# Values products of edge key blocks: 64 moved queries per head instead of 128, and a new order of the products in each stay

## The chip, the cores and the metric

The kernel runs on one core of a Trainium2 chip. The metric is device time in microseconds (us) of one execution; of several runs the median counts. The core has a matmul engine (PE in the profile; its weight loads are listed apart as PEld), VectorE (DVE), ScalarE (ACT), GpSimd (POOL) and SyncE (SP), which issues most of the DMA transfers.

## The reference

The program is a two-layer encoder over 2048 positions (prompt) and 512 positions (sample), 1024 channels, fp32. Layer 0 is windowed attention with 16 heads of 64 channels and 4 key/value heads, layer 1 a Fourier mixer; both are gated and projected, and a last RMSNorm follows. The change is in layer 0 alone. Cut to what it touches:

```
WINDOW = 128; BLOCK = 128
qb = q.reshape(b, nb, BLOCK, N_KV_HEADS, GROUP, HEAD_DIM)
kw = band_windows(k, nb)            # previous, own and next key block
vw = band_windows(v, nb)
rel = kj - BLOCK - qi               # kj in 0..383, qi in 0..127
band = np.abs(rel) <= WINDOW
scores = jnp.where(mask, scores * scale + bias, -jnp.inf)
p = jnp.exp(scores - m)
p = p / denom
o = jnp.einsum('bnhgqk,bnkhd->bnqhgd', p, vw)
```

A query block of 128 sees three key blocks (two at the ends of a sequence). The band leaves weights of zero in the first and the last of them: key j of the previous block is reached by queries 0 to j only, key j of the next block by queries j to 127 only. So the lower 64 keys of the previous block have weights other than zero only for the lower 64 queries, and the upper 64 keys of the next block only for the upper 64 queries.

## The kernel before, in words

The five chunks of 512 tokens (`CHUNKS`, line 48) are worked one after the other: first the sample, then the four of the prompt. In a chunk, layer 0 goes over 8 pairs of heads (p), and for each over two pairs of query blocks (b = 0 and 2). All products work in two parts: a number is split into a high part (rounded to the matmul's input form, `F32R`) and a low part, and a product is high x high + high x low + low x high. Where both operands have 64 rows, two products run side by side, one on rows 0 to 63 of the array and one on rows 64 to 127, writing to different PSUM banks. Such a pair is called a slot here.

For one pair of query blocks the attention steps are: scores (L650), bias and minimum on VectorE (L669), exponentials on ScalarE (L677), division (L690, L692, L696), transposes of the weights into PSUM (`transp`, L709), their split into a high part (`high`, L722, ScalarE, into `pts[:, 0]`) and a low part (`low`, L726, VectorE, into `pts[:, 1]`), the values products (`values`, L750, into `av`), and the sum of the two heads' halves (L770, L780), the gate and the split of the result (L786 to L795).

`values(b)` makes the list of products. For a query block i and a key block kb in `k0..k1` there is one for the high part of the weights and one for the low part; the values v stand with both their parts beside each other as 128 weight columns (64 channels high, 64 low), and the moving operand is `pts[rows, part, i, kb]`: 64 keys, 2 heads x 128 queries = 256 columns. The order of the list is kb ascending, high and then low in each. `half(False)` is the first stay: rows 0 to 63 of the array take all products of block 0, rows 64 to 127 all products of block 1, in turn. `half(True)`, the second stay, swaps the blocks, so that each block gets its other 64 keys; ahead of it `swapped` waits until the first stay has left the banks. A stay has 6 slots where both blocks have three key blocks. The last pair of each chunk (p = 7, b = 2) uses `whole` (L758), 128 rows at a time, and has no stays.

What stands around the stays is set by hand: `PERIOD` (line 36) and, for the first chunk, `FIRST` (line 42) list the steps of one period of two query blocks, and `seq`/`pe` chain the instructions of an engine in that order. On PE a period is AV1 (first stay), T0 (transposes of another pair of blocks), AV2 (second stay), S1 (scores), A (a run of projection products, `beside`, L524, 512 columns each), T1, S2, B (projections again). AV1 uses what `lo1`, the second low part, wrote late in the period before. `pts` has one buffer (`bufs=1`), so the next `hi0` waits for the second stay.

Of the kernel before, what the change touches and what calls it, by code (L numbers as in the profile page):

```python
# [55 lines left out]
def encoder(  # L56
# [17 lines left out]
    av = spsum.tile([P, 2, 512], F32, name="av")  # L74
# [126 lines left out]
    def pe(ins):  # L201
        return seq(PE, ins) if PE in chain else ins

    def attention_phase():

        with ExitStack() as es:
# [167 lines left out]
            vblk, k_splits = {}, []  # L374
# [151 lines left out]
            def swapped(places):  # L526

                before = []
                for last, h in places:
                    if last[1 - h] is not None:  # L530
                        before.append(last[1 - h])
                        last[1 - h] = None
                if before:
                    wait = pe(PE.nop())
                    for ins in before:
                        tc.add_manual_dep(wait.ins, ins.ins.name, DONE, reason="other rows of a bank")
# [73 lines left out]
            def attention(c, p, res, uTs):  # L610

                tok, lo_t, hi_t = CHUNKS[c]
                g = p // 2
# [24 lines left out]
                def span(b):  # L638
                    gb = tok // P + b
                    k0 = 1 if tok + b * P == lo_t else 0  # L640
                    k1 = 2 if tok + (b + 1) * P == hi_t else 3
                    return gb, k0, k1
# [85 lines left out]
                def values(b):  # L728

                    pts = st.pop("pts")  # L730
                    products, last = [], [[None, None], [None, None]]
                    for i in range(2):
                        gb, k0, k1 = span(b + i)
                        for kb in range(k0, k1):
                            v = vblk[gb - 1 + kb][:, g].rearrange("p a d -> p (a d)")
                            for part in range(2):
                                pt = pts[:, part, i, kb].rearrange("p h q -> p (h q)")
                                products.append((i, v, pt))
                    by_block = [[m for m in products if m[0] == i] for i in range(2)]

                    def half(swap):
                        todo = by_block[::-1] if swap else by_block
                        if swap:
                            swapped([(last[1], 0), (last[0], 1)])
                        for n in range(max(map(len, todo))):
                            for h in range(2):
                                if n < len(todo[h]):
                                    i, v, pt = todo[h][n]
                                    rows = slice(64 * h, 64 * h + 64)
                                    last[i][h] = pe(PE.matmul(  # L750
                                        av[:, i, :256], v[rows], pt[rows], start=not swap and n == 0,
                                        stop=swap and n == len(todo[h]) - 1, skip_group_check=True,
                                    ))

                    def whole():
                        for i, todo in enumerate(by_block):
                            for n, (_, v, pt) in enumerate(todo):
                                pe(PE.matmul(  # L758
                                    av[:, i, :256], v, pt, start=n == 0, stop=n == len(todo) - 1, skip_group_check=True
                                ))  # L760

                    st["half"] = half
                    return whole
# [42 lines left out]
                for b in (0, 2):  # L806
                    one, two = sorted((b, b + 1), key=width)
                    act = one if not c or one == b else two

                    def av1(b=b):  # L810
                        st["whole"] = values(b)
                        if (p, b) == (7, 2):
                            st.pop("half")
                            st.pop("whole")()
                        else:
                            st["half"](False)

                    def gate(b=b):
                        st["split", b] = gated(b)

                    ops[b] = {
                        "S1": lambda one=one: scores(one), "S2": lambda two=two: scores(two),
                        "b1b": lambda one=one: biased(one, 1, True), "b1a": lambda one=one: biased(one, 0, False),
                        "b2a": lambda two=two: biased(two, 0, True), "b2b": lambda two=two: biased(two, 1, False),
                        "e1a": lambda one=one: exps(one, 0), "e1b": lambda one=one: exps(one, 1),
                        "e2a": lambda two=two: exps(two, 0), "e2b": lambda two=two: exps(two, 1),
                        "r1": lambda one=one: invert(one), "r2": lambda two=two: invert(two),
                        "m1a": lambda one=one: divide(one, 0, False), "m1b": lambda one=one: divide(one, 1, True),
                        "m2a": lambda two=two: divide(two, 0, False), "m2b": lambda two=two: divide(two, 1, False),
                        "T0": lambda one=one: transp(one, 0), "T1": lambda two=two: transp(two, 1),  # L830
                        "hi0": lambda one=one: high(one), "hi1": lambda two=two: high(two),
                        "lo0": lambda one=one: low(one), "lo1": lambda two=two: low(two),
                        "AV1": av1, "AV2": second_half, "t2": lambda b=b: upper(b), "add": lambda b=b: sums(b),
                        "mul": gate, "sp": lambda b=b: split_high(b), "lop": lambda b=b: split_low(b),
                    }
# [226 lines left out]
            for c in range(len(CHUNKS)):  # L1062
# [89 lines left out]
                for n in range(19):  # L1152
# [12 lines left out]
                    order = [a for a in (PERIOD if c else FIRST) if n < 15 or a[0] not in ("hi0", "lo0")]  # L1165
# [1110 lines left out]
```

## Time and profile before

| what | value |
|---|---|
| runs | 1563.36, 1567.52 and 1564.77 us; median 1564.77 us |
| the profiled execution's own time | 1567.89 us |
| its span, first to last instruction | 1566.1 us |
| granted PE clock, mean | 0.995 of full speed |
| PE busy | 1545.2 us, 99% |
| PEld busy | 1350.9 us, 86% |
| VectorE / ScalarE / GpSimd busy | 72% / 57% / 29% |
| values products in two stays (L750) | 1680 |

The profile's page gives the busy time of each engine, then the span in 40 slices, the DMA queues, the chain of work that ended last, and groups of equal instructions with their count, their busy time, the mean duration of one, and the idle time of the engine just before them. The durations of one matmul overlap: a product is listed with 0.28 us, although the next one may start 0.12 us after it. So what a product costs is read from start to start, or from the pieces of the chain, not from its mean. PEld lies beside PE: the next weights are loaded while a product still moves its columns.

### The profile page before, as it was taken

The numbers are of one execution on the slowest core, as the hardware profiler recorded it, in microseconds if no ns is written. First come the engines' busy times: TensorE is split into PE (matmuls) and PEld (weight loads), VectorE is DVE, ScalarE is ACT, GpSimd is POOL, SyncE is SP. The second block draws the span as 40 slices with busy tenths as digits, with TensorE's granted clock in tenths as the row PEclk, the third lists the DMA queues.
The fourth block names the chain that finished last, engine by engine and source line by source line (L and its number), as shares of the span: only waits on it lengthen the run. The fifth ranks groups of instructions, "written<-read, shape, count | busy, mean of one in ns | idle before, by whom it ended". The sixth has DMA issues, their size and how long they took to land.

```text
span 1566.1 us, 33658 instructions
## 1 busy us (share of the span) xinstructions
PE 1545.2 (99%) x13150; PEld 1350.9 (86%) x13150; DVE 1123.7 (72%) x2431; ACT 889.5 (57%) x1921; POOL 450.7 (29%) x616
## 2 busy tenths in 40 slices
PE   9999999999999999999999999999999999899998
PEld 7899888999898888988888899988888888788886
DVE  5888655777637776367764577767888877889896
ACT  6788534787337784257861477746656554333353
POOL 2565662421414313314214142222112111101100
PEclk9999999999999999999999999999999999999999
DMA  9677687684856765866749666675666679456852
GB/s 330 232 264 234 222 336 280 216 293 161 297 218 220 243 232 204 302 210 205 251 136 363 232 206 224 243 257 181 223 234 218 220 242 409 149 202 250 298 191 94
DMA packets 100729, 372.70 MB, mean 238 GB/s; under 512 B 11235, under 2 KB 22251, under 8 KB 83420
## 3 DMA queue, kind: packets, MB, share of 16 engines
q1 hardware_dynamic: 82716, 297.38, 54.8%
q0 software_dynamic: 16688, 70.04, 11.5%
q10 hardware_dynamic: 1168, 3.15, 0.6%
q8 instruction: 103, 1.69, 0.4%
q14 instruction: 54, 0.44, 0.1%
HBM read 280.06 MB, written 90.47 MB: 237 GB/s over the span
## 4 chain that ended last, share of the span: by engine, by line
PE 88%; DVE 6%; DMA 3%; ACT 2%; issue 1%; POOL 0%; POOLq 0%; ACTq 0%; DVEq 0%; SPq 0%
PE pj L524 27%; PE av L750 7%; PE W L134 6%; PE pj L134 6%; PE tp L134 5%; PE av L134 5%; PE spt L650 5%; PE spt L134 4%; PE tp L709 3%; PE Wo L134 3%; PE fo L134 3%; PE Z L134 3%; PE z L1385 2%; PE Zo L134 2%; PE ABp L134 2%; PE X L134 1%
## 5 line engine op out<-in xcount | busy, mean ns | idle before, releaser
L524 PE MATMUL pj<-h,wg 64*128 64x512 f32 x1920 | 440.3, 390 | 0.0
L524 PE MATMUL pj<-h,wq 64*128 64x512 f32 x1560 | 380.4, 390 | 1.3 <-DVE qab L568 1.3
L524 PEld LDWEIGHTS pj<-h,wg 64*128 64x128 f32 x1920 | 331.5, 185 | 22.6
L524 PEld LDWEIGHTS pj<-h,wq 64*128 64x128 f32 x1560 | 285.4, 185 | 22.9 <-DVE qab L568 2.7
L669 DVE CUSTOM_DVE_ANT_0 S<-spt,b 128x385 f32<-128x385 f32 (+1 forms) x320 | 165.0, 525 | 94.1 <-PE spt L650 89.7
L677 ACT ACTIVATE S<-S 128x385 f32<-128x385 f32 (+1 forms) x320 | 189.2, 592 | 62.1 <-DVE S L669 40.5
L722 ACT CAST pts<-tp 128x768 fp32r<-128x768 f32 (+1 forms) x160 | 121.3, 758 | 96.6 <-PE av L750 59.8
L726 DVE TENSOR_TENSOR pts<-tp,pts 128x768 fp32r<-128x768 f32 (+1 forms) x160 | 144.1, 901 | 14.1 <-ACT pts L722 13.4
L750 PE MATMUL av<-pts,v 64*128 64x256 f32 x1680 | 143.7, 287 | 3.0 <-DVE pts L726 3.0
L750 PEld LDWEIGHTS av<-pts,v 64*128 64x128 f32 x1680 | 127.3, 186 | 7.3 <-DVE pts L726 3.8
L795 POOL TENSOR_TENSOR uT<-o,uT 128x256 fp32r<-128x256 f32 x75 | 56.7, 756 | 244.5 <-ACT uT L791 244.2
L650 PE MATMUL spt<-kwin,qab 64*128 64x384 f32 (+1 forms) x960 | 121.4, 339 | 0.9 <-DVE S L669 0.7
L134 PE MATMUL fo<-wo,tTu 128*128 128x512 f32 x480 | 115.7, 395 | 0.0
L134 PEld LDWEIGHTS fo<-wo,tTu 128*128 128x128 f32 x480 | 89.4, 190 | 18.1
L709 PEld LDWEIGHTS tp<-ident,S 64*128 64x128 f32 x1792 | 93.1, 137 | 10.1 <-DVE pts L726 3.1
L709 PE MATMUL tp<-ident,S 64*128 64x64 f32 x1792 | 98.0, 224 | 0.1
L786 POOL TENSOR_TENSOR o<-o,s 128x256 f32<-128x256 f32 x75 | 55.6, 742 | 120.3 <-DVE o L780 95.0
L692 DVE TENSOR_SCALAR S<-S 128x384 f32<-128x384 f32 (+1 forms) x192 | 88.5, 489 | 0.1
L650 PEld LDWEIGHTS spt<-kwin,qab 64*128 64x128 f32 x960 | 85.1, 188 | 3.8 <-issue 1.8
L279 DVE SCALAR_TENSOR_TENSOR h<-xk,g0s,h 128x512 fp32r<-128x512 f32 x40 | 45.3, 1146 | 51.3 <-ACT h L278 51.1
L524 PE MATMUL pj<-wo,uT 64*128 64x512 f32 x360 | 74.8, 390 | 0.0
L278 ACT ACTIVATE h<-xk,g0s 128x512 fp32r<-128x512 f32 x40 | 28.7, 724 | 75.2 <-POOL xk L274 75.1
(376 smaller groups left out, 3355.8 us busy)
## 6 DMA issues: line engine op xcount, KB each, us to landing
wo<-wsd SPq DMA_DIRECT2D x32, 1024.0 KB, 5.9
wq<-wsd SPq DMA_DIRECT2D x31, 1024.0 KB, 6.5
wg<-wsd SPq DMA_DIRECT2D x31, 1024.0 KB, 5.8
x<-x1d SPq DMA_DIRECT2D x40, 512.0 KB, 3.8
b<-b21d SPq DMA_DIRECT2D x40, 512.0 KB, 4.7
b<-rowd SPq DMA_DIRECT2D x40, 384.0 KB, 4.2
xs<-in_x_dram SPq DMA_DIRECT2D x23, 512.0 KB, 6.2
s2d<-gt POOLq DMA_DIRECT2D x40, 256.0 KB, 4.2
```

Source lines behind the costliest of these rows:

```text
L134: ins = pe(PE.matmul(out, a[i], b[j], start=start and i + j == 0, stop=stop and i == 1, skip_group_check=more))
L524: out.last[h] = pe(PE.matmul(out.ps, a[i], b[j], **out.flags()))
L650: pe(PE.matmul(spt[j][:, 2 + k0 * P : 2 + k1 * P], res["q"][rows, qp, b * P : (b + 1) * P], kwin[g][rows, kp, b * P + k0 * P : b * P + k1 ...
L669: seq(DVE, DVE.tensor_tensor_reduce(out=s[:, e0:e1], in0=ps[:, 1 + e0 : 1 + e1], in1=st["bias"][:, j, 386 - e1 : 386 - e0][:, ::-1], scale ...
L677: last_exp[0] = seq(ACT, ACT.activation(s[:, e0:e1], s[:, e0:e1], AF.Exp, bias=s[:, 386:387], scale=-1.0, accum_out=s[:, 387:388]))
L692: seq(DVE, DVE.tensor_scalar(s[:, ks], s[:, ks], den, None, ALU.mult))
L709: pe(PE.transpose(ps[h][:, kb, j, :], s[rows, j, 1 + kb * P : 1 + (kb + 1) * P], ident[rows, rows]))
L722: seq(ACT, ACT.copy(hi, ps))
L726: seq(DVE, DVE.tensor_tensor(lo, ps, f32(hi), ALU.subtract))
L750: last[i][h] = pe(PE.matmul(av[:, i, :256], v[rows], pt[rows], start=not swap and n == 0, stop=swap and n == len(todo[h]) - 1, skip_group_ ...
L786: eng.tensor_tensor(o, o, s, ALU.mult)
L795: low = eng.tensor_tensor(lo, o, f32(hi), ALU.subtract)
```

## The change

The list `by_block` stays for `whole`. The stays use a new list, `reached(i, h)`, for block i on row half h. Three things differ.

The key block whose 64 keys of this half reach only half of the queries (`edge`: the previous block for the lower half, the next block for the upper half) moves 2 heads x 64 queries = 128 columns, in two pieces of 64, and writes only those columns of `av`. All other products are as before. The new order is: own block high, edge high, far high, far low, edge low, own low. With it the edge products of both halves stand in the same slot where both blocks have three key blocks. And the first product of a stay, which starts the accumulation, is always one of 256 columns.

```diff
+                    def reached(i, h):
+
+                        gb, k0, k1 = span(b + i)
+                        edge, far = 2 * h, 2 - 2 * h
+                        order = [(1, 0), (edge, 0), (far, 0), (far, 1), (edge, 1), (1, 1)]
+                        rows = ahead = slice(64 * h, 64 * h + 64)
+                        out = []
+                        for kb, part in order:
+                            if k0 <= kb < k1:
+                                v = vblk[gb - 1 + kb][rows, g].rearrange("p a d -> p (a d)")
+                                pt = pts[rows, part, i, kb].rearrange("p h q -> p (h q)")
+                                to = av[:, i, :256]
+                                if kb == edge:
+                                    pt = pts[rows, part, i, kb][:, :, ahead]
+                                    to = to.rearrange("p (h q) -> p h q", h=2)[:, :, ahead]
+                                out.append((i, to, v, pt))
+                        return out
+
                     def half(swap):
-                        todo = by_block[::-1] if swap else by_block
+                        todo = [reached(h ^ swap, h) for h in range(2)]
...
-                                    i, v, pt = todo[h][n]
-                                    rows = slice(64 * h, 64 * h + 64)
+                                    i, to, v, pt = todo[h][n]
                                     last[i][h] = pe(PE.matmul(
-                                        av[:, i, :256], v[rows], pt[rows], start=not swap and n == 0,
+                                        to, v, pt, start=not swap and n == 0,
```

The number of instructions is the same on every engine, and only PE's order differs. Of the 1680 products in stays 540 are edge products; 360 of these stand in 90 stays with 6 slots and three key blocks on both sides, two slots of each stay with an edge product on both halves (180 slots); the other 180 are in the 60 stays at an end of a sequence, where the two halves have lists of unequal length.

The first place is PE, head pair 2 of the second prompt chunk, first stay. The names are the output bank pair `av`, the transposed weights `pts` and the values block `v`; the shape is what is moved through the 128 output columns. Before:

```order
L750 MATMUL av<-pts_2_0_7133,v_3_3439 128x256 [waits DVE_49,Activation_49]
L750 MATMUL av<-pts_2_0_7133,v_4_3466 128x256 [waits Activation_49]
L750 MATMUL av<-pts_2_0_7133,v_3_3439 128x256
L750 MATMUL av<-pts_2_0_7133,v_4_3466 128x256 [waits DVE_49]
L750 MATMUL av<-pts_2_0_7133,v_4_3466 128x256
L750 MATMUL av<-pts_2_0_7133,v_5_6365 128x256
```

And now, in the same place:

```order
L767 MATMUL av<-pts_2_0_7133,v_4_3466 128x256 [waits DVE_49,Activation_49]
L767 MATMUL av<-pts_2_0_7133,v_5_6365 128x256 [waits Activation_49]
L767 MATMUL av<-pts_2_0_7133,v_3_3439 128x2x64
L767 MATMUL av<-pts_2_0_7133,v_6_6368 128x2x64
L767 MATMUL av<-pts_2_0_7133,v_5_6365 128x256
L767 MATMUL av<-pts_2_0_7133,v_4_3466 128x256
L767 MATMUL av<-pts_2_0_7133,v_5_6365 128x256
L767 MATMUL av<-pts_2_0_7133,v_4_3466 128x256 [waits DVE_49]
L767 MATMUL av<-pts_2_0_7133,v_3_3439 128x2x64
```

The second wait for VectorE, that for the second block's low part, stood at the fourth product and stands at the eighth; the two edge products make up the second slot.

The second place is PE in the first chunk, head pair 2, first stay, at the beginning of the sample, where block 0 has only two key blocks. Before:

```order
L750 MATMUL av<-pts_2_0_1225,v_16_433 128x256 [waits DVE_49,Activation_49]
L750 MATMUL av<-pts_2_0_1225,v_16_433 128x256 [waits Activation_49]
L750 MATMUL av<-pts_2_0_1225,v_16_433 128x256
L750 MATMUL av<-pts_2_0_1225,v_16_433 128x256 [waits DVE_49]
L750 MATMUL av<-pts_2_0_1225,v_17_438 128x256 x4
```

And now:

```order
L767 MATMUL av<-pts_2_0_1225,v_16_433 128x256 [waits DVE_49,Activation_49]
L767 MATMUL av<-pts_2_0_1225,v_17_438 128x256 [waits Activation_49]
L767 MATMUL av<-pts_2_0_1225,v_17_438 128x256
L767 MATMUL av<-pts_2_0_1225,v_18_443 128x2x64
L767 MATMUL av<-pts_2_0_1225,v_17_438 128x256
L767 MATMUL av<-pts_2_0_1225,v_16_433 128x256 x2
L767 MATMUL av<-pts_2_0_1225,v_16_433 128x256 [waits DVE_49]
```

Here too the wait moves from the fourth product to the eighth, and the edge product of the upper half stands beside a product of 256 columns.

## The prediction

> **What bounds the kernel now.** I read the page first, then the waits of PE, then the chain and the timeline of one steady period, then the chain around the longest wait. The page's head and a few of its groups:
>
> ```profile
> span 1566.1 us, 33658 instructions
> PE 1545.2 (99%) x13150; PEld 1350.9 (86%) x13150; DVE 1123.7 (72%) x2431; ACT 889.5 (57%) x1921; POOL 450.7 (29%) x616
> ...
> PEclk9999999999999999999999999999999999999999
> ...
> L524 PE MATMUL pj<-h,wg 64*128 64x512 f32 x1920 | 440.3, 390 | 0.0
> ...
> L709 PEld LDWEIGHTS tp<-ident,S 64*128 64x128 f32 x1792 | 93.1, 137 | 10.1 <-DVE pts L726 3.1
> L709 PE MATMUL tp<-ident,S 64*128 64x64 f32 x1792 | 98.0, 224 | 0.1
> ```
>
> PE is busy for 99% of the span at the full clock, and VectorE, the next one, for 72%. So time is won where PE's slots get shorter or a wait of PE goes, and nowhere else. The row of the page on the values products shows an idle time of 3.0 us in front of all 1680; the waits of PE say how it is spread:
>
> ```profile
> L750 PE MATMUL av<-pts,v 64*128 64x256 f32 x1680 | 143.7, 287 | 3.0 <-DVE pts L726 3.0
> L750 PEld LDWEIGHTS av<-pts,v 64*128 64x128 f32 x1680 | 127.3, 186 | 7.3 <-DVE pts L726 3.8
> ```
>
> ```profile
> PE av L750 <- DVE pts L726: 3.0, 3, 1.4
> PE pj L524 <- DVE qab L568: 1.3, 4, 0.4
> ```
>
> Three waits, 1.4 us at most, for the low part that L726 writes. There is no fourth. For the price of a slot the 287 ns of the group row are of no use, as durations overlap; the pieces of the chain and the timeline of a steady period (the first column is the start, the second the time) give it. First the chain, then the timeline:
>
> ```profile
> 800.12 2.75 PE pj L524 x24
> 802.87 0.71 PE av L750 x12
> 803.58 0.37 PE tp L709 x12
> 803.96 0.79 PE av L750 x12
> ```
>
> ```profile
> 802.71 0.88 PE L750 MATMUL av<-pts,v 64*128 64x256 f32 x12
> 803.42 0.53 PE L709 MATMUL tp<-ident,S 64*128 64x64 f32 x12
> 803.76 0.96 PE L750 MATMUL av<-pts,v 64*128 64x256 f32 x12
> 804.56 0.69 PE L650 MATMUL spt<-kwin,qab 64*128 64x384 f32 x6
> 805.09 1.55 PE L524 MATMUL pj<-wo,uT 64*128 64x512 f32 x12
> ```
>
> Two products make a slot. Twelve slots of 512 columns take 2.75 us, 0.229 each; three of 384 take 805.09 - 804.56 = 0.53, 0.177 each; six of 256 take 0.71, 0.118 each; six transposes of 64 columns take 0.37, 0.062 each. The first three lie on a line of 0.055 us for 128 columns. The line alone would put a slot of 128 columns at 0.063.
>
> **What a short slot costs.** Each product also loads 128 weight columns of its own. In the timeline of the projections, the loads of the next slot start together with the products of the slot before it, one slot ahead and no more:
>
> ```profile
> 799.96 0.39 PE L524 MATMUL pj<-h,wg 64*128 64x512 f32 x1
> 799.96 0.18 PEld L524 LDWEIGHTS pj<-wo,uT 64*128 64x128 f32 x1
> ...
> 800.19 0.39 PE L524 MATMUL pj<-h,wg 64*128 64x512 f32 x1
> 800.19 0.18 PEld L524 LDWEIGHTS pj<-wo,uT 64*128 64x128 f32 x1
> ```
>
> So a slot that moves few columns may end before the next weights are in. Two places of the trace bound that load.
>
> The first is the joint of T0 and AV2, where a product of 64 columns stands ahead of a values product. From the first transpose to the first score are 804.56 - 803.42 = 1.14 us. In them lie five transposes of 0.062 (0.31), six values slots of 0.118 (0.71), and what is left, 1.14 - 0.31 - 0.71 = 0.12, is the last transpose's slot. It is twice as long as the others, though it moves the same 64 columns: what follows it is a load for a values product. That is why the second stay takes 0.79 in the chain where the first takes 0.71. By this row an edge slot costs 0.12, as much as a slot of 256.
>
> The second is the length of the loads. The smallest load of this form in the trace is that of the bias rows:
>
> ```profile
> L356 PEld LDWEIGHTS pj<-ohr,rbs 33*16 33x16 f32 x2 | 0.1, 90 | 0.4 <-issue 0.4
> ```
>
> With 16 columns it lasts 90 ns, a values load with 128 lasts 186: 96 ns for 112 columns, 0.86 ns a column, so 0.110 us for 128. The loads of the transposes (137 ns for as many columns) are cheaper, which is why their slots reach 0.062. By this estimate an edge slot costs 0.110 and saves 0.008.
>
> The Trainium skill states a rule that speaks against this change: in "TensorE: Matmul & The Clock Gate", section "LDWEIGHTS (loading the stationary operand)", a load takes the number of its columns divided by 1.2, in ns, whatever the rows. That is an estimate of 107 ns here, near the 110 of the two load rows, and the trace agrees for the values loads; for the transposes' loads it does not, since 137 ns against 186 for the same columns cannot both follow it. By the page's figure an edge slot would save 0.011 us, 3.0 us over 270 slots.
>
> **The change part by part.** Edge products: 540 of 1680 move 128 columns instead of 256. As two row halves work side by side, they are 540 / 2 = 270 slots at most; 180 of them have an edge product on both halves for certain, and only such a slot can get shorter. The gain lies between nothing (0.12 a slot, the joint) and 270 x 0.008 = 2.2 us (0.110 a slot). The joint is the nearer row: the same load, in the same place, behind a product that is even shorter. I take a quarter of the upper end, 0.5 us. All of it would be on the path, as PE is never idle in these stays. The two pieces of 64 columns in what is read and written could cost something; the transposes write 64 columns at a time at 0.062 a slot, so I put that at nothing, and its bound by the slack of the load: an edge slot has 0.118 - 0.063 = 0.055 us that its columns don't need.
>
> The order: the second wait for the low part moves from the fourth product to the eighth. In the steady period nothing waits there, as the first stay's 0.71 is six whole slots; the move buys nothing. It counts in the three waits. The timeline and the chain around the first of these:
>
> ```profile
> 68.78 0.45 PE L750 MATMUL av<-pts,v 64*128 64x256 f32 x3
> 70.56 0.61 PE L750 MATMUL av<-pts,v 64*128 64x256 f32 x5 [1.34 <-DVE pts L726]
> ```
>
> ```profile
> 67.81 0.32 DVE o L780
> ...
> 68.59 0.04 DVE S L669
> ...
> 69.07 0.56 DVE S L669 x3
> 69.64 0.88 DVE pts L726
> 70.52 0.04 issue
> 70.56 0.61 PE av L750 x5
> ```
>
> Three products are out, then PE stands for 1.34 us until VectorE has done its sums, two biased scores and the low part, and seven of the stay's ten products are left. Now seven go ahead of the wait, and three are left behind it. VectorE's end at 70.52 doesn't move, since its order is the same. So four products, two slots, go from behind the wait to under it: 2 x 0.118 x 3 waits = 0.7 us. The ends: nothing, if the transposes or scores that follow wait for VectorE in turn (it is what is late there), and 3.0 us, all the waits, which seven products instead of three can't cover. I take 0.7. The first product of a stay still waits for the high parts of both blocks, as before, and what stands behind it on PE is the same; no wait is added, and no other engine has another instruction or another order. In the second stay nothing is late: it needs the same low parts.
>
> Sum: 0.5 + 0.7 = 1.2 us. Against the profiled execution's own 1567.9 us (span 1566.1 and 1.8 around it) that is 1566.7; the median of the runs shown, 1564.8, lies 3.1 below that execution, so the forecast for the median is 1563.6 us. That is 0.08% less. About 0.3%, 4.7 us, is what a measurement of this kernel can tell from no change: the three runs alone spread over 4.2 us.
>
> **Rival one: columns set the slot, so it is faster.** If the weights of an edge slot's successor come in early enough, the line through 0.229, 0.177 and 0.118 holds down to 128 columns: 0.063 instead of 0.118, and 180 to 270 slots x 0.055 = 9.9 to 14.9 us. With 0.7 for the order that is 1549.2 to 1554.2, about 1551.7. For it speaks how straight the line is, and that transposes do run at 0.062 with a load each. Against it speak the joint's 0.12 and the 186 ns of the values' loads. It decides from 0.10 us a slot downward, where 270 slots save 4.9 us. The Trainium skill has a middle way, in the page named above, section "Back-to-back issue gap": a stream of loads and products of 128 columns in a real kernel takes about 81 ns each. As an estimate that is 0.037 less a slot and up to 10.0 us, 1554.1 with the order; no row here shows such a slot.
>
> **Rival two: a short product is not moved at the full rate, so it is slower.** Every fp32 product of this form in the trace moves 256 columns or more; none shows what 128 do. If a shorter one is done in four passes, an edge slot moves 4 x 128 = 512 column steps and costs what a slot of 512 costs, 0.229, that is 0.111 more: 180 to 270 slots x 0.111 = 20.0 to 30.0 us, 1584.1 to 1594.1 with the order, about 1589. For it speaks a little that the short transposes last longer than the line of durations says: 390 - 287 = 103 ns for 256 columns leaves 184 fixed, so 64 columns take 224 - 184 = 40 ns, 0.63 ns a column against 0.40. Against it: at 0.63 ns 128 columns take 81 ns, still hidden under a load of 110, and nothing in the rows changes its rate between 256 and 512. It decides from a slot of 0.118 + 4.7 / 270 = 0.135 us upward. The Trainium skill, "FP8 and Floating Point Precision", section "TensorE Precision Notes", knows both forms, fp32 cut to fewer bits and full fp32 in four passes; it ties neither to the number of columns, and no run here shows the four passes.
>
> **How the numbers follow.** The forecast (the load holds an edge slot at 0.11 to 0.12) gets 0.69, rival one 0.15, rival two 0.16. The forecast's own range is 1559.6 (2.2 for the slots and 3.0 for the waits) to 1568, the highest of the three runs, since a single median can lie there. It holds 0.69; with rival one it holds 0.84, so the range goes from 1549 to 1568 and leaves rival two out. Faster by over 0.3%: 0.15. Within 0.3%: 0.69. Slower: 0.16.
>
> **What would show it.** In the profile after, the groups of the values products split into 256 and 128 columns. Right: a full first stay in a steady period still takes 0.69 to 0.72 us from its first product to the first transpose, and the loads still last about 186 ns. Rival one: that stay takes 0.71 - 2 x 0.055 = 0.60. Rival two: 0.71 + 2 x 0.111 = 0.93. The order is right if the three waits for L726 are still there, each about 0.2 us shorter, with seven products ahead of them; it is wrong if they have gone, or if T0 behind them waits as much longer. A stay outside 0.67 to 0.75 makes the prediction wrong.

## The result and the profile after

The changed kernel ran at a median of 1560.07 us (eight runs, 1558.37 to 1561.51), the kernel before beside it at 1564.95 (1563.16 to 1567.52). The medians differ by 4.9 us, where 1.2 us had been forecast, and the ratio over all runs is 0.9964, 95% interval 0.9954 to 0.9974. Two more comparisons below give 0.9978 and 0.9969.

The two profiled executions differ by more, 8.7 us of span. The page after, its head and the groups that answer to those of before:

```profile
span 1557.4 us, 33658 instructions
PE 1540.8 (99%) x13150; PEld 1344.4 (86%) x13150; DVE 1126.1 (72%) x2431; ACT 889.8 (57%) x1921; POOL 450.9 (29%) x616
...
L767 PE MATMUL av<-pts,v 64*128 64x256 f32 (+1 forms) x1680 | 140.9, 284 | 2.3 <-DVE pts L726 2.3
L767 PEld LDWEIGHTS av<-pts,v 64*128 64x128 f32 x1680 | 125.3, 186 | 6.8 <-DVE pts L726 2.9
```

The idle time in front of the values products is 2.3 us instead of 3.0, and the loads still last 186 ns. The values products of the page with the forms kept apart:

```profile
L767 PE MATMUL av<-pts,v 64*128 64x256 f32 x1140 | 140.9, 314 | 2.3 <-DVE pts L726 2.3
L767 PE MATMUL av<-pts,v 64*128 64x128 f32 x540 | 72.9, 222 | 0.0
```

The 540 edge products last 222 ns each. Four passes would move as many column steps as a product of 512 columns, which is listed with 390 ns, so no short product is done in four passes. But the products of 256 columns are now listed with 314 ns instead of 287. They move as many columns as ever. The starts in the trace show why: in the full first stays of the prompt, the product behind an edge slot starts 0.07 us after it, and the next one only 0.15 us later, 0.23 for the two where it was 0.24. So a product behind an edge slot is listed early and then stands; the runs below show that it stands until its weights are there.

The timeline of a steady period, from the first stay to the scores:

```profile
527.86 0.86 PE L767 MATMUL av<-pts,v 64*128 64x256 f32 x12
528.55 0.53 PE L709 MATMUL tp<-ident,S 64*128 64x64 f32 x12
528.89 0.94 PE L767 MATMUL av<-pts,v 64*128 64x256 f32 x12
529.68 0.34 PE L650 MATMUL spt<-kwin,qab 64*128 64x384 f32 x2
```

First stay to first transpose 0.69 us (0.71 before), second stay to scores 0.79 (0.80 before). Both stays with three key blocks on each side, 12 products, got 0.01 to 0.02 us shorter, with a sixth of the moved columns gone (4 of the 12 products of a stay move half). The chain of the same profile has the first stay at 0.70, where the kernel before has 0.71:

```profile
528.02 0.70 PE av L767 x12
```

Of the three long waits two are left in the list, and the first of them looks so (the view of the waits, then the timeline):

```profile
PE av L767 <- DVE pts L726: 2.3, 2, 1.2
```

```profile
70.44 0.69 PE L767 MATMUL av<-pts,v 64*128 64x256 f32 x7
72.28 0.61 PE L767 MATMUL av<-pts,v 64*128 64x256 f32 x3 [1.15 <-DVE pts L726]
```

Seven products stand ahead of the wait, which lasts 1.15 us instead of 1.34, and three behind it. The third wait, 0.3 us before, is too short now to be listed.

What the stays and all that stands between them gained is read best from their first to their last product, since the profiles of single executions differ ahead of them and behind. The view of the line's instructions gives the first and the last start. First a second profile of the kernel before (the run b_before below, since the first one has a stretch of half clock in it, as shown further down), then the three of the changed kernel:

```profile
L750 PE MATMUL av<-pts,v x1680: 271/279/385, 51.9 to 1012.3; 64*128 64x256 f32 x187
```

```profile
L767 PE MATMUL av<-pts,v x1680: 215/277/387, 53.4 to 1010.0; 64*128 64x256 f32 x112, 64*128 64x128 f32 x75
```

```profile
L767 PE MATMUL av<-pts,v x1680: 215/277/387, 52.4 to 1008.9; 64*128 64x256 f32 x112, 64*128 64x128 f32 x75
```

```profile
L767 PE MATMUL av<-pts,v x1680: 215/277/387, 53.4 to 1009.6; 64*128 64x256 f32 x112, 64*128 64x128 f32 x75
```

960.4 us before, and 956.6, 956.5 and 956.2 after: 3.8 to 4.2 us. This stretch is called the stays' stretch below.

The rest of the 8.7 us is not the change's. The stretches of the profile of before with the granted clock (PEclk is the column behind the busy time), and the two at the same places of the program after:

```profile
88.00:97.00 9.00, 7.61 (x77) 0.81 0.84 256
1335.00:1346.00 11.00, 7.30 (x28) 0.69 0.42 146
```

```profile
88.00:97.00 9.00, 7.85 (x94) 1.00 0.79 273
1328.00:1339.00 11.00, 9.84 (x51) 1.00 0.54 150
```

Within the two stretches of before, the parts in which the clock was at half:

```profile
91.10:94.30 3.20, 3.20 (x21) 0.50 1.01 297
1337.00:1343.60 6.60, 4.90 (x16) 0.50 0.27 82
```

In the profiled execution of before the clock was halved for a while behind the second long wait and at the Fourier products at 1336 us; in that of after at neither place. PE also waits at the Fourier products, and the half clock of before begins during that wait. By the view of the waits, before and after:

```profile
PE ABp L134 <- ACT gp L1668: 4.3, 1, 4.3
```

```profile
PE ABp L134 <- ACT gp L1685: 1.2, 1, 1.2
```

So 3.1 us of the difference of the spans are in this wait. Nothing there is touched by the change, and other executions of the changed kernel have the long wait too (below).

### The profile page after: what moved, and what is told of

Read it like the earlier page. It is cut to its first block, busy times and chain, and to the rows that moved or that the text cites. A ratio compares the mean times of both kernels' runs of the same rounds, so it can differ in the third digit from the quotient of the medians.

```text
span 1557.4 us, 33658 instructions
## 1 busy us (share of the span) xinstructions
PE 1540.8 (99%) x13150; PEld 1344.4 (86%) x13150; DVE 1126.1 (72%) x2431; ACT 889.8 (57%) x1921; POOL 450.9 (29%) x616
## 4 chain that ended last, share of the span: by engine, by line
PE 89%; DVE 6%; ACT 2%; DMA 2%; issue 1%; POOL 0%; POOLq 0%; DVEq 0%; ACTq 0%; SPq 0%
PE pj L524 27%; PE av L767 7%; PE W L134 6%; PE pj L134 6%; PE tp L134 5%; PE av L134 5%; PE spt L650 5%; PE spt L134 4%; PE tp L709 4%; PE Wo L134 3%; PE fo L134 3%; PE Z L134 3%; PE z L1402 2%; PE Zo L134 2%; PE ABp L134 1%; PE X L134 1%
## 5 line engine op out<-in xcount | busy, mean ns | idle before, releaser
L722 ACT CAST pts<-tp 128x768 fp32r<-128x768 f32 (+1 forms) x160 | 121.2, 758 | 91.8 <-PE av L767 57.5
L767 PE MATMUL av<-pts,v 64*128 64x256 f32 (+1 forms) x1680 | 140.9, 284 | 2.3 <-DVE pts L726 2.3
L709 PEld LDWEIGHTS tp<-ident,S 64*128 64x128 f32 x1792 | 91.2, 137 | 10.5 <-DVE pts L726 3.2
```

The costliest lines, as they stand in the source:

```text
L709: pe(PE.transpose(ps[h][:, kb, j, :], s[rows, j, 1 + kb * P : 1 + (kb + 1) * P], ident[rows, rows]))
L722: seq(ACT, ACT.copy(hi, ps))
L767: last[i][h] = pe(PE.matmul(to, v, pt, start=not swap and n == 0, stop=swap and n == len(todo[h]) - 1, skip_group_check=True,))
```

## The experiments

All ratios are to the kernel before, run on the same chip beside them.

### The two kernels once more

The first run is the changed kernel, the second the kernel before, both without an edit.

> The changed kernel once more, beside the kernel before on the same chip. Theory (the load of the next weights holds an edge slot at about 0.11 us, three waits shortened): 3 to 3.6 us of gain in every execution from the stays and the waits, and the rest of the 4.9 us measured is stretches of half clock that the kernel before has in some executions. Then the ratio lies at 0.996 to 0.998, and the granted clock of its executions is 0.998 or so, as in the eight seen. Rival: the whole 4.9 us is in the stays; then the ratio is 0.9965 or less and the clock plays no part.

> The kernel before against itself, for the granted clock of each of its executions. Theory: ratio 1.000 within 0.001, and the clock differs from execution to execution, 0.995 to 0.998, with the longer executions at the lower clock (one stretch of 3.4 us at half speed costs 1.7 us). Rival (the clock plays no part): the clock is the same in all of them, and the times do not follow it.

Measured: the changed kernel 1561.96 us, ratio 0.9978 (0.9967 to 0.9989); the kernel before against itself 0.9992 (0.998 to 1.0004). The stays' stretch of the changed kernel is 3.9 us shorter, as in the first profile. In the twelve executions of the kernel before, five had a granted clock of 0.999, with a median of 1561.49 us, and seven one of 0.996 to 0.998, six of them from 1565 to 1567 us. The changed kernel had its shortest times, 1557.34 and 1557.59, at 0.999 too, and four with a median of 1562.78 at 0.997. So either kernel spreads over some 5 us, the longer executions at the lower clock; that is more than the change is worth, and at the same clock the two stand 3 to 4 us apart. In this profile of the changed kernel the wait that had been 1.2 us is

```profile
PE ABp L134 <- ACT gp L1685: 3.4, 1, 3.4
```

which shows that the long form of it is not the kernel before's alone.

> The changed kernel a third time, for its ratio. Theory: 3.5 us of gain (0.9978) give or take the stretches of half clock. Rival (all of the first comparison's 4.9 us is the change's): 0.9965 or less.

Measured: 1559.13 us, ratio 0.9969 (0.9959 to 0.998), with the clock at 0.999 in seven of twelve executions. The three ratios have a mean of 0.9970, 4.6 us. The first theory's 3.5 us is a little low, the rival's 4.9 is the upper end; the stays' stretch says 3.8 to 4.2.

### One half of the change at a time

The narrow edge products alone:

```diff
-                        order = [(1, 0), (edge, 0), (far, 0), (far, 1), (edge, 1), (1, 1)]
+                        order = [(1, 0), (1, 1), (edge, 0), (edge, 1), (far, 0), (far, 1)]
```

> The edge products move 128 columns as in the changed kernel and stand in one slot on both halves, but the low part of the own block comes second again, so the wait for the low part is back at the fourth product. Theory: a full first stay behind projections takes 0.698 us as in the changed kernel, against 0.715; the three waits are as long as before, and the kernel is about 2.5 us faster than before, 0.7 us or so slower than the changed one. Rival (the order brings the gain): 0.715 a stay and no gain.

The new order alone:

```diff
-                                if kb == edge:
-                                    pt = pts[rows, part, i, kb][:, :, ahead]
-                                    to = to.rearrange("p (h q) -> p h q", h=2)[:, :, ahead]
```

> The new order alone: all products of the stays move 256 columns. Theory: a full first stay takes 0.715 us as before; the three waits shrink by about 0.24 us each; 0.7 us faster than before at most, ratio 0.999 to 1.000. Rival (the order brings the gain, by shorter waits and so fewer stretches of half clock): 2 us or more faster, ratio 0.9985 or less.

Measured: narrow alone 1562.53 us, ratio 0.9985 (0.9976 to 0.9995); order alone 1560.91 us, ratio 0.9987 (0.9977 to 0.9998). The stays' stretch, narrow alone and then order alone:

```profile
L767 PE MATMUL av<-pts,v x1680: 217/278/386, 52.0 to 1010.3; 64*128 64x256 f32 x129, 64*128 64x128 f32 x58
```

```profile
L764 PE MATMUL av<-pts,v x1680: 274/279/383, 51.9 to 1010.5; 64*128 64x256 f32 x187
```

958.3 and 958.6 us: 2.1 us for the narrow products, 1.8 for the order, together 3.9, which is what both do at once. The chain has the first stay at 0.70 us with the narrow products and at 0.71 with the order alone:

```profile
536.49 0.70 PE av L767 x12
```

```profile
536.04 0.71 PE av L764 x12
```

The waits for the low part, in the same sequence:

```profile
PE av L767 <- DVE pts L726: 3.0, 3, 1.4
```

```profile
PE av L764 <- DVE pts L726: 2.3, 2, 1.2
```

They are those of before with the narrow products and those of the changed kernel with the order, so the three long waits are worth the 0.7 us of the forecast. By its ratio the order alone gains 2 us, with an interval of 0.3 to 3.6, so the comparison does not tell theory (0.7 at most) and rival (2 or more) apart.

Where the other 1.1 us of the order lie is seen when the stretch is split at the chunks, from the first start of a values product in a chunk to the last. Between the first and the second chunk no values product runs. There the profile of the order alone has 91.2 us and that of the kernel before 91.8, while the three profiles of the changed kernel have 91.5 to 91.8. Executions of one kernel differ there, so these 0.6 us cannot be put down to the order. In the chunks themselves the order gains 1.3 us: 0.65 in the first chunk, where the three waits are, and 0.6 in the four of the prompt together, where the two profiles of the kernel before differ by 0.1. The full first stays there are as long as before; what got shorter instead is not shown.

By chunks the narrow products alone gain 1.9 us and the changed kernel 4.0 in each of its three profiles. So it is partly chance that 2.1 and 1.8 add up to 3.9: by chunks the parts make 3.2, some 0.8 us come only with both at once, and the runs do not say how.

### Is it the load?

Edge products of 32 columns:

```diff
-                                    pt = pts[rows, part, i, kb][:, :, ahead]
-                                    to = to.rearrange("p (h q) -> p h q", h=2)[:, :, ahead]
+                                    few = slice(64 * h, 64 * h + 16)
+                                    pt = pts[rows, part, i, kb][:, :, few]
+                                    to = to.rearrange("p (h q) -> p h q", h=2)[:, :, few]
```

> As the changed kernel, but an edge product moves 2 x 16 = 32 columns instead of 2 x 64 (it leaves out the products of 48 of the 64 queries per head, so that part of the weighted sum is missing). Theory (the load of the next weights sets an edge slot): nothing changes, a full first stay behind projections still takes 0.698 us and the kernel is within 1 us of the changed one. Rival (columns set what the edge slot takes): 96 columns less at 0.055 us for 128 are 0.041 a slot, so the stay takes 0.616 us and the kernel is 7 to 11 us faster than the changed one.

Measured: 1560.59 us, ratio 0.9971 (0.996 to 0.9982), the changed kernel's own time. The group of the edge products, and the first stay in the chain:

```profile
L768 PE MATMUL av<-pts,v 64*128 64x32 f32 x540 | 60.5, 181 | 0.0
```

```profile
536.01 0.69 PE av L768 x12
```

With a quarter of the columns a product lasts 181 ns instead of 222, and the stay is 0.69 instead of 0.70. Columns below 128 buy next to nothing.

Five of the six products of a stay with 128 columns:

```diff
-                                if kb == edge:
+                                if (kb, part) != (1, 0):
```

> As the changed kernel, but all products of a stay except the first move 128 columns (it leaves out half of the queries in the other key blocks). Theory: each narrow slot saves 0.008 to 0.009 us as the edge slots do, so a full first stay takes about 0.67 us (0.715 - 5 x 0.009), and the kernel is 3 to 4 us faster than the changed one. Rival (columns set the slot): 0.715 - 5 x 0.055 = 0.44 us a stay, some 30 us faster than the kernel before.

Measured: 1556.11 us, ratio 0.995 (0.9933 to 0.9967). The first stay:

```profile
533.98 0.62 PE av L767 x12
```

0.62, not the 0.67 of the theory and far from the rival's 0.44. The theory's working had left out what stands behind the stay: the last narrow slot is followed by a transpose, whose load is short (137 ns against 186), so it can shrink to its columns. One slot of 0.118, four of 0.110 and one of 0.063 make 0.621. This was worked out after the run; no run tests it by itself.

Lighter loads behind the edge slots:

```diff
                                     to = to.rearrange("p (h q) -> p h q", h=2)[:, :, ahead]
+                                elif (kb, part) in ((far, 0), (1, 1)):
+                                    v, to = v[:, :96], av[:96, i, :256]
```

> As the changed kernel, but the two products of a stay that stand right behind an edge slot load 96 weight columns instead of 128 (it leaves out half of the low part of the values in these two products). Theory: an edge slot is as long as the load behind it, so at 0.86 ns a column it gets 32 x 0.86 = 0.027 us shorter; a full first stay takes 0.698 - 2 x 0.027 = 0.644 us, and the kernel is 5 to 7 us faster than the changed one. Rival (the floor of an edge slot is something else, such as a fixed cost of a product): 0.698 us, no gain.

Measured: 1553.3 us, ratio 0.9936 (0.9915 to 0.9957). The two kinds of loads, and the first stay:

```profile
L769 PEld LDWEIGHTS av<-pts,v 64*128 64x128 f32 x1110 | 101.2, 186 | 7.1 <-DVE pts L726 3.0 <-ACT S L690 0.3
L769 PEld LDWEIGHTS av<-pts,v 64*96 64x96 f32 x570 | 60.6, 159 | 0.0
```

```profile
531.89 0.64 PE av L769 x12
```

The loads are 27 ns shorter, the stay is 0.64 us, as the theory had it, although not one product moves fewer columns than in the changed kernel. By the starts in the trace, an edge slot and the one behind it take 0.20 us together instead of 0.23. This settles the cause: the weight columns of the load behind an edge slot set its length, 32 of them for 0.027 us.

### Versions built on it

High and low part of an edge product through one load. One product moves both parts, 256 columns; VectorE adds the low part's result:

```diff
-                        order = [(1, 0), (edge, 0), (far, 0), (far, 1), (edge, 1), (1, 1)]
+                        order = [(1, 0), (far, 0), (edge, 0), (far, 1), (1, 1)]
...
-                                    pt = pts[rows, part, i, kb][:, :, ahead]
-                                    to = to.rearrange("p (h q) -> p h q", h=2)[:, :, ahead]
+                                    pt = pts[rows, :, i, kb][:, :, :, ahead]
+                                    to = av[:, i].rearrange("p (e h q) -> p e h q", e=2, h=2)[:, :, :, ahead]
...
+                            to = t2[:, blocks, :, qs]
+                            seq(DVE, DVE.tensor_tensor(to, to, low[:, blocks, :, qs], ALU.add))
```

> A version built on the theory: if a slot of 128 columns costs nearly as much as one of 256, the high and the low part of an edge product should go through one load. One product moves 64 queries x 2 heads x 2 parts = 256 columns, the low part's result goes to the unused half of the bank and VectorE adds it in one more sum per pair of blocks. A full stay has 5 slots instead of 6. Theory: the first stay takes 0.715 - 0.118 = 0.595 us or so; 90 full stays are worth 10.6 us and the 60 others up to 7 us against the kernel before: 1548 to 1555 us, ratio 0.990 to 0.994. Rival (the added sum, about 0.7 us on VectorE in each of 75 pairs of blocks, comes on the path, as the banks come free later): half or more of that is lost, 1556 us or more.

Measured: 1553.72 us, ratio 0.9932 (0.9914 to 0.995), inside the theory's range. The chain has both stays, and the waits of PE:

```profile
533.74 0.59 PE av L767 x10
534.33 0.37 PE tp L709 x12
534.70 0.65 PE av L767 x10
```

```profile
PE av L767 <- DVE pts L726: 3.6, 7, 1.3
```

0.59 for five slots, as expected. The stays' stretch is 11.1 us shorter (949.3) where 150 stays with a slot less of 0.118 would have made 17.7 if all had three key blocks on both sides. The rival has a small part in what is missing: there are seven waits for the low part instead of two, 3.6 us instead of 2.3. Another part is not the version's: this profile has half clock from 90.6 to 94.0 us, and the same in the first profile of the kernel before made its stretch 962.0 us instead of 960.4.

Light loads for all products of the low part, with narrow edges:

```diff
...
-                        order = [(1, 0), (edge, 0), (far, 0), (far, 1), (edge, 1), (1, 1)]
+                        order = [(1, 0), (far, 0), (edge, 0), (far, 1), (edge, 1), (1, 1)]
+                        if swap:
+                            order = [(1, 1), (1, 0), (far, 0), (edge, 0), (edge, 1), (far, 1)]
...
+                                if part:
+                                    v, to = v[:, :72], to[:72]
```

> Narrow edge products as in the changed kernel, and all products of the low part of the weights load 72 columns (64 for the values' high part, 8 more; it leaves out low part x low part, which the split products elsewhere in the kernel leave out too). The order is such that behind an edge slot a light load follows: own, far, edge high, then far, edge, own low; the second stay begins with own low. Theory: a light load takes 72 x 0.86 = 0.062 us, so an edge slot shrinks to its columns, 0.063; a full first stay takes 4 x 0.118 + 2 x 0.063 = 0.60 us, the second, whose first load is light, 0.63 to 0.65; the kernel runs 1543 to 1549 us. Rival (the floor of about 0.11 stays whatever is loaded): 0.698 and 0.784 as in the changed kernel, about 1561 us.

The same without the narrow edges:

```diff
-                                if kb == edge:
-                                    pt = pts[rows, part, i, kb][:, :, ahead]
-                                    to = to.rearrange("p (h q) -> p h q", h=2)[:, :, ahead]
                                 if part:
                                     v, to = v[:, :72], to[:72]
```

> The control: light loads and order as in the run before, but all products move 256 columns. Theory: a slot of 256 is set by its columns, so the first stay takes 0.715 us as before the change; only the second gains at its first load, 0.795 to about 0.745; with the three waits 2 to 4.5 us faster than before. Rival (the light loads bring the gain by themselves): most of the gain of the run before.

Measured: light and narrow 1544.85 us, ratio 0.9873 (0.9853 to 0.9893); light and wide 1557.62 us, ratio 0.9961 (0.9942 to 0.9979). The chain of the first, then of the second:

```profile
527.54 0.61 PE av L771 x12
528.14 0.37 PE tp L709 x12
528.52 0.61 PE av L771 x12
```

```profile
525.58 0.71 PE av L768 x12
526.29 0.37 PE tp L709 x12
526.66 0.71 PE av L768 x12
```

With light loads and wide products the first stay is 0.71 as before the change; the second is 0.71 too, where it had been 0.79, since its first load, behind the short transposes, is now light. With narrow edges both are 0.61. The pieces of the chain run from end to end; by the starts, over the steady periods of the prompt, the second stay takes 0.79 us before, 0.74 with light loads and 0.64 with narrow edges as well, as the theory had it (0.745, and 0.63 to 0.65). That the first stay remains at 0.71 with light loads also shows that the fewer output rows of these products do not shorten a slot by themselves. So narrow products alone are worth 2.1 us in the stays' stretch, light loads alone (with the order) 5.4 (955.0), and both together 20.3 (940.1): each takes away one of two limits, and only both at once let the slot shrink. The load of 72 columns, in the run with narrow edges:

```profile
L771 PEld LDWEIGHTS av<-pts,v 64*72 64x72 f32 x840 | 61.0, 141 | 3.0 <-DVE pts L726 3.0
```

The version with both is 0.9% faster than the changed kernel and the best of the study. It leaves out only products of low part x low part.

## Why the prediction was right, and where it was off

The main step was right: the load of the next weights, not the columns, holds an edge slot, and 540 products at half the columns are worth only about 2 us, 0.13%. The full first stay, forecast at 0.69 to 0.72, is 0.69 to 0.70. The time lies in the range, but that says little: the range goes from 1549 to 1568 and would hold a kernel with no gain as well, and 4.9 us came where 1.2 had been forecast. Rival one (0.60) fell, its middle way too (two slots with 0.037 less would make 0.64), and so did rival two (0.93): from 32 to 128 columns a product's 181 ns grow to 222, 0.43 ns a column, near the 0.40 of the wide ones.

Two terms of the sum were too small.

The term of the slots, 0.5 us, is 2.1 in the stays' stretch (1.9 in the chunks). The step that failed is "The joint is the nearer row". It put the slot at 0.12, a number left over from a subtraction of 0.31 and 0.71 from 1.14, all rounded to 0.01, as large as what was to be told apart. With the mean starts of the steady periods of that trace, 1.138 and 0.717, the same subtraction leaves 0.11. The other row, the length of the loads, gave 0.110 and an upper end of 2.2 us, and that is what came: the model 4 x 0.118 + 2 x 0.110 = 0.692 against 0.69 to 0.70 measured, and 0.64 and 0.62 in the runs with lighter loads and with five narrow slots, from the same 0.86 ns a column. The loads of 72, 96 and 128 columns last 141, 159 and 186 ns, 0.80 ns more for each column. The Trainium skill's rule in "TensorE: Matmul & The Clock Gate", section "LDWEIGHTS (loading the stationary operand)", makes 0.83 ns a column. The traces agree for these loads in what a column adds, not in the whole listed time (186 ns, where the rule has 107), and the prediction's estimate by that rule, 3.0 us over 270 slots, is nearer to the 2.1 than the 0.5 taken.

The term of the order, 0.7 us, is 1.3 in the chunks. For the three waits it was right, 3.0 us to 2.3, with seven products ahead as forecast; the third wait, 0.3 us long before, has gone from the list only because it was that short. The step that failed is "In the steady period nothing waits there", by which "the move buys nothing" outside the three waits: 0.6 us more came in the four prompt chunks, and no wait of the profile names them. Their cause stays open, as does that of the 0.8 us that come only with both halves of the change.

And the median of a comparison moves by a further microsecond or so with the stretches of half clock and the wait that comes with one of them, which the forecast had only as the spread of three runs. Ratios of 0.9964, 0.9978 and 0.9969 for one kernel lie on both sides of the 0.3%, so whether this counts as "within 0.3%", to which the forecast gave 0.69, or as "faster", 0.15, is not settled by any one of them; the work on the stays themselves, 4 us, is 0.25%.

## What to carry to other kernels

In these stays a product cost the longer of its own columns and the load behind it. So before halving the columns of a product, compare them with the next load: here 256 columns were worth 0.118 us and a load of 128 weight columns 0.110, and a slot of halved products bought about 0.008 us. Where a narrow product is wanted, make the load behind it small as well (fewer weight columns, or an instruction with a cheap load behind it): the two together gave 20.3 us, where the narrow products alone gave 2.1 and the light loads with their order 5.4. And when two rows of a profile bound a price, take the one that was measured directly over the one that is left from a subtraction.

## What the runs showed of the hardware

- The load of a values product gets longer by about 0.8 ns with each weight column (141, 159 and 186 ns for 72, 96 and 128), and that of a transpose with the same 128 columns takes only 137 ns in all. Among the slots with loads of 128 columns, those of the transposes take 0.062 us (0.37 us for six slots of two), and those of values products with such a load behind them took about 0.11, whether they moved 128 columns or 32.
- The granted clock can be halved behind a wait of PE of little over 1 us, in some executions and not in others: it was 0.50 of full speed over 3.2 us behind the second long wait (1.39 us) in the first profile of before, and not behind the same wait in the second profile.
- At the Fourier products, the seven kept profiles in which PE waits for 2.35 to 4.33 us have half clock there, beginning during the wait or up to 1.4 us after it, and the six with 1.16 to 2.04 us have none. Executions of the kernel before spread from 1561 to 1567 us, the longer ones at the lower mean clock. Since the wait and the half clock come together, the runs do not say how much of the spread is due to each.
